# The last norm of a transformer layer: weights multiplied on VectorE before the row factor, the factor applied on ScalarE

## The chip, the cores and the metric

The kernel runs on one core of a Trainium2 chip. The metric is the device time of one execution in microseconds (us), as the median of several runs. Within a core TensorE (PE in the profile) multiplies matrices into PSUM, VectorE (DVE), ScalarE (ACT) and GpSimd (POOL) do elementwise work, SyncE (SP) issues the transfers. Each engine takes its instructions strictly in the order of its own queue, and engines wait for each other by semaphores.

## The reference

One layer of an encoder on two sequences (a prompt and a sample) of 512 rows by 1024 columns. What matters here is the end: the second half of the MLP, a gated residual add, and the final RMS norm.

```python
x = x + g2 * (jnp.square(jax.nn.relu(h @ w_mlp1)) @ w_mlp2)
return rms_norm(x, final_g)      # (x * rsqrt(mean(x*x, -1) + 1e-6)) * final_g
```

`g2` is one gate value per column and sequence, `final_g` one weight per column. The norm therefore multiplies each element by a factor of its row (known only once the whole row is finished) and by a weight of its column (known from the start).

## The kernel before

The product with `w_mlp2` is done by a seven-product scheme on 2x2 blocks, so the output is split into four quarters (i, j): i picks a half of the rows, j a half (512) of the columns. Each row half has four tiles of 128 rows, t = 0..3; tiles 0 and 1 belong to the prompt, 2 and 3 to the sample. In the program's last group of steps the products come in the order P1, P2, P6, P7, P4, P5, P3. The quarter (0,0) is complete after P2, (1,0) after P4, (1,1) after P5 and (0,1) after P3.

Each factor is split into a high and a low part: `prep` casts the high parts on ScalarE (line 841) and subtracts them on VectorE for the low parts (line 842, 128x1024, four of these for a product; `uc` are the left factors, `wc` the right ones). `multiply` (line 1310) then issues 12 matmuls for a product and a row tile, four chunks by three pairs of parts. P1, P6, P5 and P3 run in the PSUM bank pairs `x` (one pair for tiles 0 and 1, one for tiles 2 and 3), P2, P7 and P4 in `y`. The next matmuls into a pair wait until VectorE has read what stood there: (P5, tile 1) waits for the read of (P5, tile 0), (P3, 0) for that of (P5, 1), (P3, 1) for that of (P3, 0), and in the same way for the tiles 2 and 3.

Products that complete no quarter are added into SBUF tiles `acc` (`gather`), and `gated_sums` multiplies these by the gate (line 1349) and adds them to the rows `x2r` (line 1350). A product that completes a quarter goes through `gated_bank`: VectorE reads the bank times the gate into `acc` (line 1356) and adds this to `x2r` (line 1357). `squares` then sums the squares of a tile's 512 columns on ScalarE (line 1362) and GpSimd turns the sum into the mean (line 1365). `finish` has GpSimd raise it to the power -1/2 (line 1369, `rf`), VectorE multiplies each half of the row by the factor and the column weights `fgain` in one instruction (line 1373, SCALAR_TENSOR_TENSOR), and SyncE stores each half (line 1374).

The order of instructions within each engine's queue is set when the kernel is built by a scheduler that goes by dependences and its own costs; at run time it is fixed. So what is written in one place of the code may stand elsewhere in a queue. In the names below, `x2r_0_9503`, `x2r_1_9505`, `x2r_2_9507` and `x2r_3_9509` are the tiles 0 to 3 of row half 1; `x2r_0_9511` to `x2r_3_9517` are those of row half 0. `fgain_9347` are the weights of column half 0, `fgain_9353` those of column half 1. `uc_3` and `wc_3` belong to P7, `uc_5` and `wc_5` to P4, `uc_4` and `wc_4` to P5, `uc_6` and `wc_6` to P3.

Of the kernel before, what the change touches and what calls it, by code (L numbers as in the profile page):

```python
# [12 lines left out]
AF = mybir.ActivationFunctionType  # L13
ALU = mybir.AluOpType

P = 128
# [14 lines left out]
def trunk_kernel(ctx, tc, x0, x1, c0, c1, w_ada, b_ada, norm1_g, w_in, attn_sink, decay_f, decay_b,  # L31
                 w_out, norm2_g, w_mlp1, w_mlp2, final_g, y0, y1):
    nc = tc.nc
    xin = (x0[0], x1[0])
    yout = (y0[0], y1[0])
# [25 lines left out]
    def f2(name, dtype=F32):  # L61
        return work.tile([P, 512], dtype, tag="f2", name=name, bufs=8)

    def junk(name):
        return work.tile([P, 1024], BF16, tag="f2", name=name, bufs=8)

    def small(shape, name, tag="small", bufs=24):
        return work.tile(shape, F32, tag=tag, name=name, bufs=bufs)
# [246 lines left out]
    def x_rstd(b, t, xt):  # L315
        ssq = small([P, 1], f"ssq_{b}_{t}")
        nc.scalar.activation(junk(f"jk_{b}_{t}"), xt, AF.Square, accum_out=ssq)
        return rms_rstd(ssq, f"x_{b}_{t}")
# [511 lines left out]
    P1, P2, P6, P7, P5, P4, P3 = range(7)  # L830
# [9 lines left out]
    def split_to(hi, lo, src):  # L840
        nc.scalar.copy(hi, src)  # L841
        nc.vector.tensor_sub(lo, src, f(hi))  # L842
# [21 lines left out]
    class FirstPair:  # L864
# [15 lines left out]
        def prep(self, p):  # L880
            r1, r2 = self.raw
            c = lambda t: t.rearrange("p (s k n) -> p s k n", s=2, n=P)
            w = lambda t: t.rearrange("p (k n) -> p k n", n=256)
            F1, F2 = slice(0, P), slice(P, 256)
            if p in (P1, P2):
                t = c(self.pair(f"a{p}", True))
                split_to(t[:, 0], t[:, 1], (r1 if p == P1 else r2)[:, :, F1])
                self.left[p] = t[:, 0], t[:, 1]
            elif p == P6:
                self.s1 = f2(f"ws1_{self.n}").rearrange("p (k n) -> p k n", n=P)  # L890
                nc.vector.tensor_tensor(self.s1, r1[:, :, F2], r2[:, :, F2], ALU.add)
                nc.vector.tensor_sub(r1[:, :, F2], r1[:, :, F1], r1[:, :, F2])
                nc.vector.tensor_sub(r1[:, :, F1], self.s1, r1[:, :, F1])
                h, l = w(self.pair("s2h", False)), w(self.pair("s2l", False))
                split_to(h, l, r1)
                self.left[P6] = h[:, :, F1], l[:, :, F1]
                self.left[P7] = h[:, :, F2], l[:, :, F2]
            elif p == P5:
                t = c(self.pair("s1", True))
                split_to(t[:, 0], t[:, 1], self.s1)  # L900
                self.left[P5] = t[:, 0], t[:, 1]
            elif p == P4:
                nc.vector.tensor_sub(r2[:, :, F1], r2[:, :, F1], r1[:, :, F1])
                h, l = w(self.pair("s4h", False)), w(self.pair("s4l", False))
                split_to(h, l, r2)
                self.left[P3] = h[:, :, F1], l[:, :, F1]
                self.left[P4] = h[:, :, F2], l[:, :, F2]
# [162 lines left out]
    r0 = x_rstd(0, 0, xt0[0])  # L1070
# [189 lines left out]
    acc, fin = {}, {}  # L1260
# [65 lines left out]
    def cols_of(j):  # L1326
        return slice(j * 512, (j + 1) * 512)


    def final_loads():  # L1330
        for j in range(2):
            for b in range(NB):
                fin["g", b, j] = f2(f"fgate_{b}_{j}")
                in_order(nc.sync.dma_start(fin["g", b, j], gates[NB + b:NB + b + 1, cols_of(j)].broadcast_to([P, 512])))
            fin["f", j] = f2(f"fgain_{j}")
            in_order(nc.sync.dma_start(fin["f", j], final_g[cols_of(j)].rearrange("(o d) -> o d", o=1).broadcast_to([P, 512])))
# [15 lines left out]
    def gated_bank(q, t, src):  # L1352

        a = acc[q, t // 2][:, t % 2, :]
        x = fin["x", q[0], t][:, cols_of(q[1])]
        nc.vector.tensor_tensor(a, src, fin["g", t // 2, q[1]], ALU.mult)  # L1356
        nc.vector.tensor_tensor(x, x, a, ALU.add)

    def squares(q, t):
        i, j = q  # L1360
        ss = small([P, 1], f"ssf_{i}_{t}_{j}")
        nc.scalar.activation(junk(f"jkf_{i}_{t}_{j}")[:, :512], fin["x", i, t][:, cols_of(j)], AF.Square, accum_out=ss)
        before = fin.get(("ms", i, t), EPS)
        ms = fin["ms", i, t] = small([P, 1], f"msf_{i}_{t}_{j}")
        nc.gpsimd.tensor_scalar(ms, ss, 1.0 / D, before, ALU.mult, ALU.add)

    def finish(i, t):
        r = small([P, 1], f"rf_{i}_{t}")
        nc.gpsimd.tensor_tensor(r, fin["ms", i, t], neghalf[:, 0:1], ALU.pow)
        x = fin["x", i, t]  # L1370
        r0 = i * 256 + (t % 2) * P
        for j in range(2):
            nc.vector.scalar_tensor_tensor(x[:, cols_of(j)], x[:, cols_of(j)], r, fin["f", j], ALU.mult, ALU.mult)
            nc.sync.dma_start(yout[t // 2][r0:r0 + P, cols_of(j)], x[:, cols_of(j)])


    ahead = {P1: lambda: (load_w(0, 0, 0), load_u(0, P1)),
# [26 lines left out]
    def loads(s):  # L1404
        if 2 < s < len(steps):
            load_u(*steps[s])

    def weights(s):
        if 2 < s < len(steps):
            g, p = steps[s]  # L1410
            for k, j in blocks.get(p, ()):
                load_w(g, k, j)

    for s, (g, p) in enumerate(steps[:-2]):
        loads(s + 2)
        weights(s + 3)
        final = g == ng - 1
        if final and p == P1:
            final_loads()
        if s + 1 < len(steps) and s > 0:  # L1420
            prep(*steps[s + 1])
        for t in range(4):
            src = multiply(g, p, t)
            if final and p == P4:
                gated_bank((1, 0), t, src[:, t % 2, :])
                squares((1, 0), t)
            elif t % 2 == 1:
                gather(p, t // 2, src)
        if final:
            if p == P2:  # L1430
                final_rows(1)
                final_rows(0)
            elif p == P6:
                gated_sums((1, 0))
                gated_sums((0, 0))
            elif p == P7:
                gated_sums((1, 1))
                gated_sums((0, 1))
                for t in range(4):
                    squares((0, 0), t)  # L1440
    prep(*steps[-1])
    g = ng - 1
    for p, t in ((P5, 0), (P5, 1), (P3, 0), (P5, 2), (P3, 1), (P5, 3), (P3, 2), (P3, 3)):
        src = multiply(g, p, t)
        q = where[p]
        gated_bank(q, t, src[:, t % 2, :])
        squares(q, t)
        finish(q[0], t)
    lates.close()
    front.close()  # L1450

# [26 lines left out]
```

## Time and profile before

| | |
|---|---|
| runs before | 1161.26 us median of 3 (1159.34 to 1162.54) |
| profiled execution | 1161.89 us, of which its span 1160.1 us |
| busy: PE, DVE, ACT, POOL | 96%, 80%, 43%, 6% of the span |
| granted TensorE clock, mean | 0.992 |
| last group's end on PE | about 1149.7 us |
| last elementwise instruction (line 1373) | starts 1155.44 us, two of them take 1.42 us |

Busy shares are means over the whole program; the change concerns its last 80 us or so. A row of the timeline gives the start, the duration, the engine, the line, the operation and its tiles, and in brackets how long the engine had been idle and what released it. `x5` at the end of a row means that many instructions in a row. One instruction may start before the one ahead of it has ended, so the pitch, from start to start, is somewhat shorter than the duration.

### The profile page before, as it was taken

How to read it: one execution, taken by the hardware profiler on the slowest of the kernel's cores; microseconds unless marked ns; L12 is line 12 of the kernel's file. 1: busy time of each engine (PE TensorE's matmuls, PEld its weight loads, DVE VectorE, ACT ScalarE, POOL GpSimd, SP SyncE). 2: the span in 40 equal slices, each digit the busy share in tenths (PEclk: the TensorE clock that was granted, in tenths of full speed). 3: DMA queues.
4: the chain of work that ended last, by engine and by line, in shares of the span. 5: the costliest groups of instructions: out<-in, count | busy, mean ns of one | idle time of the engine just before them, and what ended most of it. 6: DMA issues, size and time to landing. Idle time of an engine off the chain costs nothing.

```text
span 1160.1 us, 14470 instructions
## 1 busy us (share of the span) xinstructions
PE 1109.4 (96%) x5167; PEld 903.8 (78%) x5167; DVE 933.4 (80%) x1550; ACT 494.0 (43%) x846; POOL 69.0 (6%) x79
## 2 busy tenths in 40 slices
PE   5899999999999999999999999999999999999975
PEld 3578787777888788888788888888778888888854
DVE  5888988978888697689998778866696866968896
ACT  4456765435563234346333333332455333432341
POOL 3620001000000000000000000000000000000012
PEclk9999999999999999999999999999999999999988
DMA  9796677655455489941654455443866364464413
GB/s 289 238 283 211 214 230 272 218 193 190 155 167 199 156 303 333 343 148 46 214 204 155 164 165 189 155 163 103 287 230 237 106 195 137 144 200 139 184 37 145
DMA packets 124112, 224.37 MB, mean 193 GB/s; under 512 B 8500, under 2 KB 59780, under 8 KB 124040
## 3 DMA queue, kind: packets, MB, share of 16 engines
q1 hardware_dynamic: 111144, 217.14, 55.8%
q10 hardware_dynamic: 12544, 6.29, 1.9%
q8 instruction: 40, 0.66, 0.3%
q0 software_dynamic: 352, 0.03, 0.1%
q14 instruction: 32, 0.26, 0.1%
HBM read 152.36 MB, written 71.06 MB: 193 GB/s over the span
## 4 chain that ended last, share of the span: by engine, by line
PE 75%; DVE 11%; DMA 5%; issue 3%; ACT 3%; POOL 2%; SPq 0%; ACTq 0%; DVEq 0%; POOLq 0%
PE px_None L936 12%; PE x L1310 12%; PE py_None L936 9%; PE y L1310 9%; PE po L129 2%; PE po L130 2%; PE po L128 2%; DMA raw_ada_g<-in_w_ada_dram 2%; PE po L429 1%; PE ppt L422 1%; PE psc L396 1%; PE pj_rq L129 1%; PE pj_rq L128 1%; PE pj_rv L128 1%; PE pj_rv L130 1%
## 5 line engine op out<-in xcount | busy, mean ns | idle before, releaser
L841 ACT CAST uc_0h<-ur 128x1024 fp32r<-128x1024 f32 x28 | 29.4, 1050 | 67.9 <-PE x L1310 38.1
L1310 PE MATMUL x<-wc_0l,uc_0h 128*128 128x512 f32 x128 | 50.7, 396 | 5.4 <-DVE wc_0l L842 5.4
L1310 PE MATMUL x<-wc_0h,uc_0h 128*128 128x512 f32 x128 | 50.5, 396 | 3.9 <-DVE acc L1356 3.2
L128 PE MATMUL po<-wh_wo,ms 128*128 128x512 f32 x128 | 50.5, 397 | 1.9 <-ACT ms L761 1.9
L1310 PE MATMUL x<-wc_1h,uc_1h 128*128 128x512 f32 x128 | 50.3, 394 | 1.0 <-ACT wc_1h L841 1.0
L1310 PE MATMUL x<-wc_1l,uc_1h 128*128 128x512 f32 x128 | 50.2, 392 | 0.5 <-DVE wc_1l L842 0.5
L1310 PE MATMUL x<-wc_0h,uc_0l 128*128 128x512 f32 x128 | 50.3, 393 | 0.0
L1310 PE MATMUL x<-wc_1h,uc_1l 128*128 128x512 f32 x128 | 50.1, 391 | 0.0
L129 PE MATMUL po<-wl_wo,ms 128*128 128x512 f32 x128 | 49.8, 391 | 0.3 <-DVE wl_wo L103 0.3
L842 DVE TENSOR_TENSOR uc_0l<-ur,uc_0h 128x1024 fp32r<-128x1024 f32 x28 | 34.2, 1222 | 19.6 <-ACT uc_0h L841 15.9
L130 PE MATMUL po<-wh_wo,ms 128*128 128x512 f32 x128 | 49.6, 390 | 0.0
L255 DVE SCALAR_TENSOR_TENSOR adacc_c<-raw_ada_c,cact,adacc_c 128x512 f32<-128x512 f32 x56 | 39.8, 748 | 6.7 <-DMA raw_ada_c<-in_w_ada_dram 5.7
L841 ACT CAST wc_s4h<-raw_w 128x1024 fp32r<-128x1024 f32 x16 | 16.8, 1053 | 62.8 <-PE px_None L936 46.1
L406 ACT ACTIVATE st<-st,negm 128x256 f32<-128x256 f32 (+1 forms) x64 | 35.2, 556 | 18.8 <-DVE negm L401 18.8
L841 ACT CAST wc_0h<-w 128x1024 fp32r<-128x1024 f32 x24 | 25.2, 1049 | 42.4 <-DVE w L1289 16.3
L255 DVE SCALAR_TENSOR_TENSOR adacc_g<-raw_ada_g,cact,adacc_g 128x512 f32<-128x512 f32 x56 | 40.3, 747 | 2.1 <-DMA raw_ada_g<-in_w_ada_dram 1.8
L842 DVE TENSOR_TENSOR wc_0l<-w,wc_0h 128x1024 fp32r<-128x1024 f32 x24 | 29.3, 1221 | 13.5 <-ACT wc_0h L841 13.4
L936 PE MATMUL py_None<-hch,wc_a 128*128 128x512 f32 x120 | 39.7, 390 | 0.1
L936 PE MATMUL px_None<-hch,wc_a 128*128 128x512 f32 x120 | 39.6, 391 | 0.0
L936 PE MATMUL px_None<-hch,wc_s 128*128 128x512 f32 x120 | 39.4, 389 | 0.0
L1310 PE MATMUL y<-wc_1l,uc_1h 128*128 128x512 f32 x96 | 37.5, 391 | 0.6 <-DVE wc_1l L842 0.6
L1310 PE MATMUL y<-wc_0h,uc_0h 128*128 128x512 f32 x96 | 37.6, 392 | 0.0
(397 smaller groups left out, 3484.8 us busy)
## 6 DMA issues: line engine op xcount, KB each, us to landing
ur<-spill SPq DMA_DIRECT2D x56, 512.0 KB, 4.3
raw_w<-in_w_mlp_dram SPq DMA_DIRECT2D x32, 512.0 KB, 3.8
spill<-s SPq DMA_DIRECT2D x64, 256.0 KB, 3.7
w<-in_w_mlp_dram SPq DMA_DIRECT2D x32, 512.0 KB, 5.4
spill<-u SPq DMA_DIRECT2D x48, 256.0 KB, 2.3
raw_ada_g<-in_w_ada_dram SPq DMA_DIRECT2D x16, 512.0 KB, 4.3
raw_ada_c<-in_w_ada_dram SPq DMA_DIRECT2D x16, 512.0 KB, 4.0
raw_ada<-in_w_ada_dram SPq DMA_DIRECT2D x12, 512.0 KB, 8.8
```

The source lines that it names most:

```text
L128: nc.tensor.matmul(ps, lhs[0], rhs[0], start=start, stop=False)
L129: nc.tensor.matmul(ps, lhs[0], rhs[1], start=False, stop=False)
L130: nc.tensor.matmul(ps, lhs[1], rhs[0], start=False, stop=stop)
L255: nc.vector.scalar_tensor_tensor(acc[b], src, cb, acc[b], ALU.mult, ALU.add)
L396: nc.tensor.matmul(psc[:, :w], qs[hh][:, isl], k_[:, s, j0 * P:j1 * P], start=(s == 0), stop=(s == 1))
L406: nc.scalar.activation(st[hh][:, :w], st[hh][:, :w], AF.Exp, bias=negm[:, hh:hh + 1], scale=0.125, accum_out=den[:, hh:hh + 1])
L422: nc.tensor.transpose(pt[:, hh * P:(hh + 1) * P], st[hh][:, jj * P:(jj + 1) * P], ident)
L429: nc.tensor.matmul(po, va[:, j0 + jj, g].rearrange("p s e -> p (s e)"), pts[jj][:, s, :], start=(jj == 0 and s == 0), stop=(jj == nj - 1 a ...
L841: nc.scalar.copy(hi, src)
L842: nc.vector.tensor_sub(lo, src, f(hi))
L936: self.last = nc.tensor.matmul(bank[:, cs], x[:, k, :], y, start=first and k == 0 and i == 0, stop=last and k == 3 and i == 2, skip_group_ ...
L1310: nc.tensor.matmul(out, u[x][:, i % 2, ts_], w[y][:, i % 2, :], start=first and i == 0 and k == 0, stop=end and i == GP - 1 and k == 2, sk ...
```

## The change

The norm's two multiplications are separated. `gained` multiplies a half row by the column weights on VectorE, as a TENSOR_TENSOR, as soon as that half's sum of squares is taken or its rows are complete, before the row factor exists. The factor is then applied by ScalarE, as an ACTIVATE (Copy) with the factor as its scale, once for each half; only the last half of the last tile takes a TENSOR_SCALAR on VectorE. For column half 1 the weighted rows go to the `acc` tile, so that the squares can be read from `x2r` meanwhile.

```diff
-    def finish(i, t):
+    def gained(q, t, dst):
+
+        nc.vector.tensor_tensor(dst, fin["x", q[0], t][:, cols_of(q[1])], fin["f", q[1]], ALU.mult)
+
+    def finish(i, t, last):
+
+        a = acc[(i, 1), t // 2][:, t % 2, :]
+        gained((i, 1), t, a)
         r = small([P, 1], f"rf_{i}_{t}")
         nc.gpsimd.tensor_tensor(r, fin["ms", i, t], neghalf[:, 0:1], ALU.pow)
-        x = fin["x", i, t]
         r0 = i * 256 + (t % 2) * P
-        for j in range(2):
-            nc.vector.scalar_tensor_tensor(x[:, cols_of(j)], x[:, cols_of(j)], r, fin["f", j], ALU.mult, ALU.mult)
-            nc.sync.dma_start(yout[t // 2][r0:r0 + P, cols_of(j)], x[:, cols_of(j)])
+        for j, src in ((0, fin["x", i, t][:, cols_of(0)]), (1, a)):
+            if j == 1 and last:
+                nc.vector.tensor_scalar(src, src, r, None, ALU.mult)
+            else:
+                nc.scalar.activation(src, src, AF.Copy, scale=r)
+            nc.sync.dma_start(yout[t // 2][r0:r0 + P, cols_of(j)], src)
...
                 for t in range(4):
                     squares((0, 0), t)
+            elif p == P4:
+                for t in range(4):
+                    gained((0, 0), t, fin["x", 0, t][:, cols_of(0)])
     prep(*steps[-1])
+    for t in range(4):
+        gained((1, 0), t, fin["x", 1, t][:, cols_of(0)])
...
-        finish(q[0], t)
+        finish(q[0], t, (p, t) == (P3, 3))
```

VectorE's queue at the end of P6's step, ahead of the low parts for P7 (a minus is a row of before alone, a plus of after alone):

```order
 L1350 TENSOR_TENSOR x2r_0_9511<-x2r_0_9511,acc_0_7810 128x512
 L1350 TENSOR_TENSOR x2r_0_9511<-x2r_0_9511,acc_0_8267 128x512
-L1350 TENSOR_TENSOR x2r_1_9513<-x2r_1_9513,acc_0_7810 128x512
+L1369 TENSOR_TENSOR x2r_0_9511<-x2r_0_9511,fgain_9347 128x512
 L1324 TENSOR_TENSOR acc_0_7963<-x_0_0_9371,acc_0_7963 128x1024
 L842 TENSOR_TENSOR uc_3_0l<-ur_3_0_9423,uc_3_0h 128x1024
```

The first of the new multiplications takes the place of one residual add, and that add now stands 13 rows further down, among the other adds of line 1350 and ahead of all low parts of P4 and P5:

```order
 L1350 TENSOR_TENSOR x2r_2_9507<-x2r_2_9507,acc_1_7989 128x512
 L1350 TENSOR_TENSOR x2r_3_9509<-x2r_3_9509,acc_1_7989 128x512
+L1350 TENSOR_TENSOR x2r_1_9513<-x2r_1_9513,acc_0_7810 128x512
 L1350 TENSOR_TENSOR x2r_2_9515<-x2r_2_9515,acc_1_7837 128x512
 L1350 TENSOR_TENSOR x2r_3_9517<-x2r_3_9517,acc_1_7837 128x512
```

VectorE's queue of before from P3's second low part to the first reads of P5's banks (the last two rows):

```order
L842 TENSOR_TENSOR wc_6_0l<-w_3_11_0_9269,wc_6_0h 128x1024
L1356 TENSOR_TENSOR acc_0_7963<-y_3_0_9627,fgate_0_9343 128x512
L842 TENSOR_TENSOR uc_6_1l<-ur_6_1_9717,uc_6_1h 128x1024
L1357 TENSOR_TENSOR x2r_1_9505<-x2r_1_9505,acc_0_7963 128x512
L1356 TENSOR_TENSOR acc_1_7989<-y_3_1_9653,fgate_0_9345 128x512
L842 TENSOR_TENSOR wc_6_1l<-w_3_11_1_9271,wc_6_1h 128x1024
L1357 TENSOR_TENSOR x2r_3_9509<-x2r_3_9509,acc_1_7989 128x512
L1356 TENSOR_TENSOR acc_0_8036<-x_0_0_9371,fgate_1_9349 128x512
L1356 TENSOR_TENSOR acc_1_8063<-x_0_1_9397,fgate_1_9351 128x512
```

The same stretch of the changed kernel, to the same two rows; three more rows of line 1369, for the tiles 1 to 3 of row half 0, stand right ahead of it:

```order
L1356 TENSOR_TENSOR acc_0_7963<-y_3_0_9627,fgate_0_9343 128x512
L842 TENSOR_TENSOR uc_6_0l<-ur_6_0_9715,uc_6_0h 128x1024
L1357 TENSOR_TENSOR x2r_1_9505<-x2r_1_9505,acc_0_7963 128x512
L1356 TENSOR_TENSOR acc_1_7989<-y_3_1_9653,fgate_0_9345 128x512
L842 TENSOR_TENSOR wc_6_0l<-w_3_11_0_9269,wc_6_0h 128x1024
L1357 TENSOR_TENSOR x2r_3_9509<-x2r_3_9509,acc_1_7989 128x512
L842 TENSOR_TENSOR uc_6_1l<-ur_6_1_9717,uc_6_1h 128x1024
L842 TENSOR_TENSOR wc_6_1l<-w_3_11_1_9271,wc_6_1h 128x1024
L1369 TENSOR_TENSOR x2r_0_9503<-x2r_0_9503,fgain_9347 128x512
L1369 TENSOR_TENSOR x2r_1_9505<-x2r_1_9505,fgain_9347 128x512
L1369 TENSOR_TENSOR x2r_2_9507<-x2r_2_9507,fgain_9347 128x512
L1369 TENSOR_TENSOR x2r_3_9509<-x2r_3_9509,fgain_9347 128x512
```

The reads of P5's banks follow right behind, so seven multiplications by the weights now stand between the first reads of P4's banks and the first read of P5's. On PE the matmuls are the same in number; those of (P5, tile 3) are spread over three gaps between the others (4, 4, 4) in place of two (7, 5).

ScalarE's queue at the end of before holds only sums of squares:

```order
L1362 ACTIVATE jkf_2_1_9917,ssf_2_1_9916<-x2r_2_9507 128x512
L1362 ACTIVATE jkf_1_1_9942,ssf_1_1_9941<-x2r_1_9513 128x512
L1362 ACTIVATE jkf_3_1_9967,ssf_3_1_9966<-x2r_3_9509 128x512
L1362 ACTIVATE jkf_2_1_9992,ssf_2_1_9991<-x2r_2_9515 128x512
L1362 ACTIVATE jkf_3_1_10017,ssf_3_1_10016<-x2r_3_9517 128x512
```

In the changed kernel each of these is followed by the two products with the row factor, which wait for GpSimd's `rf`, and the next tile's squares stand behind them:

```order
L1362 ACTIVATE jkf_1_1_9954,ssf_1_1_9953<-x2r_1_9513 128x512
L1382 ACTIVATE x2r_1_9513<-x2r_1_9513,rf_1_9959 128x512
L1382 ACTIVATE acc_0_8267<-acc_0_8267,rf_1_9959 128x512
L1362 ACTIVATE jkf_3_1_9980,ssf_3_1_9979<-x2r_3_9509 128x512
L1382 ACTIVATE x2r_3_9509<-x2r_3_9509,rf_3_9985 128x512
L1382 ACTIVATE acc_1_8063<-acc_1_8063,rf_3_9985 128x512
L1362 ACTIVATE jkf_2_1_10006,ssf_2_1_10005<-x2r_2_9515 128x512
L1382 ACTIVATE x2r_2_9515<-x2r_2_9515,rf_2_10011 128x512
L1382 ACTIVATE acc_1_8293<-acc_1_8293,rf_2_10011 128x512
L1362 ACTIVATE jkf_3_1_10032,ssf_3_1_10031<-x2r_3_9517 128x512
L1382 ACTIVATE x2r_3_9517<-x2r_3_9517,rf_3_10037 128x512
```

VectorE's queue then ends with the read, the add and the weights of the last tile, and one TENSOR_SCALAR (line 1380); no instruction of it but this last waits for GpSimd. SyncE's 16 stores wait for ScalarE in place of VectorE.

## Prediction

> **What bounds the kernel now.** The page first: its own time 1161.89 us, span 1160.1. I then cut the last 73 us into stages. The columns are busy time and instructions of PE, its weight loads, DVE, ACT and POOL, the clock, and the transfers.
>
> ```profile
> 1087.00:1120.00 33.00, 26.98 (x109) 21.24 (x108) 32.78 (x41) 13.06 (x18) 1.20 (x3) 0.91 0.21 64
> 1120.00:1130.00 10.00, 9.60 (x41) 7.56 (x40) 8.95 (x12) 5.73 (x11) 2.84 (x4) 0.95 0.00 1
> 1130.00:1150.00 20.00, 16.92 (x71) 12.71 (x69) 15.02 (x23) 4.84 (x14) 6.58 (x14) 1.00 0.29 109
> 1150.00:1160.00 10.00, 0.00 (x0) 0.00 (x0) 4.96 (x8) 0.72 (x2) 1.48 (x3) 0.59 0.54 202
> ```
>
> From 1087 to 1120 VectorE is busy 32.78 of 33 us: any instruction put there moves everything behind it. ACT is nearly free, which speaks for the change. Next, who waits for whom from 1110 on (total, times, longest):
>
> ```profile
> PE x L1310 <- DVE wc_0l L842: 5.4, 1, 5.4
> PE x L1310 <- DVE acc L1356: 3.2, 4, 1.8
> DVE x2r L1373 <- POOL rf L1369: 6.7, 5, 1.9
> ```
>
> PE waits 5.4 us for P5's low part and 3.2 us for reads of its banks; VectorE stands 6.7 us in front of the row factor, with the next bank's read queued behind. The timeline places these. VectorE up to the first read of P5's banks:
>
> ```profile
> 1119.20 1.30 DVE L1357 TENSOR_TENSOR x2r<-x2r,acc 128x512 f32<-128x512 f32 x2
> 1120.40 1.23 DVE L842 TENSOR_TENSOR uc_0l<-ur,uc_0h 128x1024 fp32r<-128x1024 f32 x1
> 1123.61 0.69 DVE L1356 TENSOR_TENSOR acc<-y,fgate 128x512 f32<-128x512 f32 x1 [0.68 <-PE y L1310]
> 1126.33 0.69 DVE L1356 TENSOR_TENSOR acc<-y,fgate 128x512 f32<-128x512 f32 x1 [0.29 <-PE y L1310]
> 1126.94 1.22 DVE L842 TENSOR_TENSOR wc_1l<-w,wc_1h 128x1024 fp32r<-128x1024 f32 x1
> 1128.07 0.69 DVE L1357 TENSOR_TENSOR x2r<-x2r,acc 128x512 f32<-128x512 f32 x1
> 1128.67 1.28 DVE L1356 TENSOR_TENSOR acc<-x,fgate 128x512 f32<-128x512 f32 x2
> ```
>
> These give the pitches: 0.60 us for a 128x512 TENSOR_TENSOR (1128.07 to 1128.67), 1.13 for a 128x1024 one (1126.94 to 1128.07), and only 0.97 us of idle time in all. PE in the same stretch and on to its end:
>
> ```profile
> 1115.88 0.79 PE L1310 MATMUL x<-wc_0l,uc_0h 128*128 128x512 f32 x1 [5.42 <-DVE wc_0l L842]
> 1116.47 0.63 PE L1310 MATMUL x<-wc_0h,uc_0l 128*128 128x512 f32 x1
> 1116.90 0.63 PE L1310 MATMUL x<-wc_0h,uc_0h 128*128 128x512 f32 x1
> ...
> 1121.10 0.40 PE L1310 MATMUL y<-wc_0h,uc_0l 128*128 128x512 f32 x1
> ...
> 1128.62 0.39 PE L1310 MATMUL x<-wc_1h,uc_1l 128*128 128x512 f32 x1
> 1129.41 0.50 PE L1310 MATMUL x<-wc_0h,uc_0h 128*128 128x512 f32 x1 [0.40 <-DVE acc L1356]
> ...
> 1134.66 0.47 PE L1310 MATMUL x<-wc_0h,uc_0h 128*128 128x512 f32 x1 [0.65 <-DVE acc L1356]
> 1139.18 0.50 PE L1310 MATMUL x<-wc_0h,uc_0h 128*128 128x512 f32 x1 [0.38 <-DVE acc L1356]
> 1146.70 0.50 PE L1310 MATMUL x<-wc_0h,uc_0h 128*128 128x512 f32 x1 [1.77 <-DVE acc L1356]
> 1147.04 0.39 PE L1310 MATMUL x<-wc_0l,uc_0h 128*128 128x512 f32 x1
> 1147.27 0.40 PE L1310 MATMUL x<-wc_0h,uc_0l 128*128 128x512 f32 x1
> 1149.33 0.39 PE L1310 MATMUL x<-wc_1h,uc_1l 128*128 128x512 f32 x1
> ```
>
> PE's last matmul ends at 1149.72. After the idle 5.42 us the starts lie 0.43 apart (1116.47 to 1116.90) until about 1121.10; after the idle 1.77 us they are at once 0.23 apart. Lastly the end, from all engines:
>
> ```profile
> 1146.17 0.63 ACT L1362 ACTIVATE jkf<-x2r 128x512 bf16<-128x512 f32 x1 [4.86 <-DVE x2r L1357]
> 1147.59 0.55 POOL L1369 TENSOR_TENSOR rf<-msf,neghalf 128x1 f32<-128x1 f32 x1
> 1148.17 4.08 DVE L1373 SCALAR_TENSOR_TENSOR x2r<-x2r,rf,fgain 128x512 f32<-128x512 f32 x6 [0.80 <-POOL rf L1369]
> 1152.17 0.68 DVE L1356 TENSOR_TENSOR acc<-x,fgate 128x512 f32<-128x512 f32 x1
> 1152.88 0.69 DVE L1357 TENSOR_TENSOR x2r<-x2r,acc 128x512 f32<-128x512 f32 x1
> 1153.69 0.63 ACT L1362 ACTIVATE jkf<-x2r 128x512 bf16<-128x512 f32 x1 [5.48 <-DVE x2r L1357]
> 1155.44 1.42 DVE L1373 SCALAR_TENSOR_TENSOR x2r<-x2r,rf,fgain 128x512 f32<-128x512 f32 x2 [1.87 <-POOL rf L1369]
> ```
>
> The last bank is read at 1152.17, 2.45 us after PE's end, because six instructions of line 1373 stand ahead of it.
>
> **The change part by part.** (1) One residual add leaves a place where VectorE waited for PE anyway and goes into the full stretch before 1120; the weights' product that takes its place fits the idle time. So P5's low part, and PE with it, come 0.60 us later: 1116.48 in place of 1115.88.
>
> (2) Seven weights' products now lie ahead of the first read of P5's banks: 7 x 0.60 = 4.2 us. The reads of P4's last banks wait for PE, which is 0.60 later too. Queue by queue: three products from 1121.0 to 1122.8, then the wait for PE's y until 1124.2 (1123.61 + 0.6); read, low part, add to 1126.5; the next y at 1126.9; read, low part, add, two low parts, four products (0.60 + 1.13 + 0.60 + 2 x 1.13 + 4 x 0.60 = 7.0) to 1133.9. The first read of P5 starts there in place of 1128.67, 5.2 us later. PE has nothing else: it is through with its earlier work at 1128.85 + 0.60 = 1129.45 and starts (P5, 1) at 1134.65 in place of 1129.41: +5.2, an idle time of about 5.1 us where it was 0.40.
>
> (3) From there PE has the same 72 matmuls. VectorE no longer waits for the factor, so three of the four waits change: before, 0.65 + 0.38 + 1.77 = 2.8 us. After, four matmuls of (P5, 3) cover the read for (P3, 0) and (P3, 1); (P3, 2) waits about 1.2 for the read of (P5, 3), which stands two instructions behind that of (P3, 1), and (P3, 3) about 0.8 for the read of (P3, 2). Together 2.0: -0.8. PE ends at 1149.72 + 5.2 - 0.8 = 1154.1.
>
> (4) The last bank is read at once, at 1154.2 in place of 1152.17: +2.0. Of the 5.2 us lost, 3.2 are given back by (3) and (4).
>
> (5) ScalarE now holds, for each tile, the squares, a wait for the factor, and two products, and the next squares stand behind. Squares to factor is 1.75 us (1153.69 to 1155.44) and 2.0 where VectorE runs beside GpSimd (1146.17 to 1148.17). For a product of ScalarE by a column of factors the nearest rows are these (two of the timeline, then groups by line):
>
> ```profile
> 1085.60 1.04 ACT L841 CAST uc_0h<-ur 128x1024 fp32r<-128x1024 f32 x1
> 1086.54 0.62 ACT L1362 ACTIVATE jkf<-x2r 128x512 bf16<-128x512 f32 x1
> ...
> L253 ACT ACTIVATE adacc_g<-raw_ada_g,cact 128x512 f32<-128x512 f32 x8 | 5.6, 720 | 7.1 <-DMA raw_ada_g<-in_w_ada_dram 7.1
> L808 DVE TENSOR_SCALAR x<-x,rr_x 128x1024 f32<-128x1024 f32 x8 | 6.0, 753 | 3.9 <-DMA x2s<-x 2.0 <-POOL rr_x L306 2.0
> ```
>
> So 0.72, and about 0.63 from start to start: the cast above runs 1.04 and is followed after 0.94, an overlap of 0.1 that I take over. A tile takes ScalarE 1.75 to 2.0 + 2 x 0.63 = 3.0 to 3.3 us, and the last four, behind (P3, 0) and (P5, 2), which come as a pair, have no room between them. They fall behind VectorE by 0.6 (chain 1.75) to 1.4 us (chain 2.0). I take the middle, +1.0, as both kinds of rows occur. Bounds: zero if ScalarE keeps up, and +2 if every product costs its full 0.72.
>
> (6) At the end two instructions of line 1373 in a row (1.42) become 0.72 on ScalarE beside a TENSOR_SCALAR on VectorE, half the 0.75 of the 128x1024 row above, about 0.4. That is -0.7, or -0.3 if the two stores, now issued together, share the transfer engines; -0.5. Their queue, SyncE's, holds nothing else.
>
> Sum without the clock: +2.0 + 1.0 - 0.5 = +2.5.
>
> (7) The clock. The nearest rows for an idle time of 5.1 us are 5.42 (slow afterwards) and 1.77 (not); 5.1 lies by the first. The slow spell of before took 5.22 us for the twelve starts from 1115.88 to 1121.10, where 12 x 0.23 = 2.7 would do: 2.4 us lost, by its length rather than the work. It falls on (P5, 1), which nothing hides, as VectorE waits for it. Taken: +2.4; the bounds are 0 and 2.5.
>
> Sum: +4.9, so 1166.8 on the profiled execution. That stood 0.63 above the median shown: 1166.2, I say 1166.
>
> [...]
>
> **The rivals.** *The stall without the slow clock.* The same wait, but the matmuls after it at 0.23: 1161.26 + 2.5 = 1163.8. For it: 5.1 is shorter than the one idle time that is seen to slow PE, and nothing between 1.77 and 5.42 is seen. Against: it is far nearer to 5.42. *ScalarE becomes the bound.* Its chains run at 3.3 us and more, products at 0.72 or beside GpSimd delays: 1.5 us on top, 1167.7 with the slow clock. Against: ACT was busy 4.84 of 20 us. *Faster.* The seven products stay hidden: VectorE reaches the read of (P5, 0) before PE has done its other work at 1129.45. Then the 2.8 us of waits fall to 2.0, the 2.45 at the end and 0.5 more are gone: 1161.26 - 3.7 = 1157.5. It decides at 4.2 us of slack in VectorE's queue ahead of 1128.67, and the rows show 0.97; against it. *The change does nothing here*: losses and gains cancel, 1161.3, as when the wait in (2) were 2.5 us shorter; the same rows speak against that.
>
> **How the numbers follow.** Slow clock 0.50, stall without it 0.28, ScalarE bound 0.09, faster 0.06, cancelling 0.07. A measurement tells about 0.3%, 3.5 us, from no change, that is 1157.8 to 1164.7. Slower: nearly all of the first and third and a seventh of the second, 0.61; faster 0.05; the rest, 0.34, the same. The range reaches from 1162.6 (the second case with ScalarE keeping up) to 1168.4 (the third with its bounds); the likeliest alone is 1164.8 to 1167.4.
>
> **What would show it.** Right: PE idle about 5 us in front of (P5, 1) with line 1356 as its releaser; starts 0.43 apart behind it; the last read right at PE's end; ScalarE's last squares late for `rf` of the tile ahead. Wrong: the seven instructions of line 1369 well under 0.60 us each, an idle time there under 3 us, or ACT's products far from 0.63.

## The result and the profile after

| | before | after |
|---|---|---|
| median of 6 runs each, same chip | 1161.11 us (1159.34 to 1165.30) | 1167.49 us (1167.17 to 1169.12) |
| profiled execution, its span | 1161.89, 1160.1 us | 1167.19, 1165.4 us |

The change makes the kernel slower: ratio 1.0052, 95% interval 1.0040 to 1.0064, or 6.4 us by the medians.

Two executions have to be set side by side first. A gather that waits for a bank of PE marks how far the program was; this one stands right behind the first of the new multiplications. Timeline of before, VectorE:

```profile
1087.22 1.22 DVE L1324 TENSOR_TENSOR acc<-x,acc 128x1024 f32<-128x1024 f32 x1 [1.08 <-PE x L1310]
```

The same instruction after the change:

```profile
1085.80 1.22 DVE L1324 TENSOR_TENSOR acc<-x,acc 128x1024 f32<-128x1024 f32 x1 [0.80 <-PE x L1310]
```

The profiled execution of after came there 1.42 us earlier. It came just as much earlier to the gather in front of that multiplication (1080.36 in place of 1081.78), so this first multiplication costs nothing. From here on this is added to its times: the spans differ by 5.3 us, but from this place on by 1165.4 + 1.42 - 1160.1 = 6.7 us, which is near the 6.4 of the medians.

Busy time by stage, after (columns: PE, its weight loads, DVE, ACT, POOL, the clock, transfers):

```profile
1087.00:1120.00 33.00, 26.51 (x105) 20.69 (x104) 33.00 (x43) 12.49 (x20) 1.86 (x3) 0.91 0.22 64
1130.00:1150.00 20.00, 15.11 (x54) 11.56 (x55) 14.25 (x23) 8.64 (x18) 5.32 (x11) 0.83 0.27 100
```

VectorE's last 0.2 us of room ahead of 1120 are gone. From 1130 to 1150 the clock is 0.83 where it was 1.00, and PE is busy for 1.8 us less. Who waits for whom from 1110 on:

```profile
ACT x2r L1382 <- POOL rf L1376: 9.3, 7, 1.9
PE x L1310 <- DVE acc L1356: 7.1, 3, 5.1
```

The 6.7 us that VectorE waited for the factor have become 9.3 us of ScalarE's, and PE's waits for reads of banks went from 3.2 to 7.1 us, 5.1 of them in one place. VectorE up to the first read of P5's banks:

```profile
1119.61 1.89 DVE L1369 TENSOR_TENSOR x2r<-x2r,fgain 128x512 f32<-128x512 f32 x3
1123.20 0.69 DVE L1356 TENSOR_TENSOR acc<-y,fgate 128x512 f32<-128x512 f32 x1 [1.70 <-PE y L1310]
...
1130.54 2.49 DVE L1369 TENSOR_TENSOR x2r<-x2r,fgain 128x512 f32<-128x512 f32 x4
1132.95 1.28 DVE L1356 TENSOR_TENSOR acc<-x,fgate 128x512 f32<-128x512 f32 x2
```

The seven products by the weights stand in two groups, three ahead of P4's reads and four ahead of P5's. PE behind them:

```profile
1115.08 0.79 PE L1310 MATMUL x<-wc_0l,uc_0h 128*128 128x512 f32 x1 [5.42 <-DVE wc_0l L842]
...
1133.68 0.80 PE L1310 MATMUL x<-wc_0h,uc_0h 128*128 128x512 f32 x1 [5.08 <-DVE acc L1356]
...
1137.69 0.61 PE L1310 MATMUL x<-wc_1h,uc_1h 128*128 128x512 f32 x1
1138.12 0.41 PE L1310 MATMUL x<-wc_1l,uc_1h 128*128 128x512 f32 x1
1138.37 0.39 PE L1310 MATMUL x<-wc_1h,uc_1l 128*128 128x512 f32 x1
...
1148.54 0.50 PE L1310 MATMUL x<-wc_0h,uc_0h 128*128 128x512 f32 x1 [1.21 <-DVE acc L1356]
1152.34 0.50 PE L1310 MATMUL x<-wc_0h,uc_0h 128*128 128x512 f32 x1 [0.78 <-DVE acc L1356]
...
1155.00 0.39 PE L1310 MATMUL x<-wc_1h,uc_1l 128*128 128x512 f32 x1
```

After 5.08 us of idle time ten starts lie 0.43 apart, then 0.23 again. Two short waits follow, and PE ends at 1155.39. The end, from all engines:

```profile
1155.42 0.61 ACT L1362 ACTIVATE jkf<-x2r 128x512 bf16<-128x512 f32 x1
1155.43 0.69 DVE L1356 TENSOR_TENSOR acc<-x,fgate 128x512 f32<-128x512 f32 x1 [1.69 <-PE x L1310]
...
1156.15 0.69 DVE L1357 TENSOR_TENSOR x2r<-x2r,acc 128x512 f32<-128x512 f32 x1
1156.22 0.75 POOL L1365 TENSOR_SCALAR msf<-ssf,msf 128x1 f32<-128x1 f32 x1 [2.08 <-ACT jkf L1362]
1156.88 0.69 DVE L1369 TENSOR_TENSOR acc<-x2r,fgain 128x512 f32<-128x512 f32 x1
1157.06 0.92 POOL L1376 TENSOR_TENSOR rf<-msf,neghalf 128x1 f32<-128x1 f32 x1
1158.01 0.72 ACT L1382 ACTIVATE x2r<-x2r,rf 128x512 f32<-128x512 f32 x1 [1.89 <-POOL rf L1376]
...
1159.25 0.61 ACT L1362 ACTIVATE jkf<-x2r 128x512 bf16<-128x512 f32 x1
...
1160.40 0.55 POOL L1376 TENSOR_TENSOR rf<-msf,neghalf 128x1 f32<-128x1 f32 x1
1160.99 0.72 ACT L1382 ACTIVATE x2r<-x2r,rf 128x512 f32<-128x512 f32 x1 [1.03 <-POOL rf L1376]
1160.99 0.49 DVE L1380 TENSOR_SCALAR acc<-acc,rf 128x512 f32<-128x512 f32 x1 [3.42 <-POOL rf L1376]
```

The last bank is read at once. Its row is complete at 1156.84 (1156.15 + 0.69), but the last Square starts at 1159.25: ScalarE first has the Square, the wait for the factor and the products of the tile ahead (1155.42 to 1159.25, 3.83 us). Beside VectorE's lines 1357 and 1369 GpSimd's mean takes 0.75 us and the factor 0.92; beside nothing the two take 0.26 (at 1160.06) and 0.55.

### The profile page after: what moved, and what is told of

Read it like the earlier page. It is cut to its first block, busy times and chain, and to the rows that moved or that the text cites. A ratio compares the mean times of both kernels' runs of the same rounds, so it can differ in the third digit from the quotient of the medians.

```text
span 1165.4 us, 14486 instructions
## 1 busy us (share of the span) xinstructions
PE 1111.6 (95%) x5167; PEld 905.3 (78%) x5167; DVE 933.0 (80%) x1551; ACT 503.7 (43%) x861; POOL 72.1 (6%) x79
## 4 chain that ended last, share of the span: by engine, by line
PE 76%; DVE 11%; DMA 4%; issue 3%; ACT 3%; POOL 2%; SPq 0%; ACTq 0%; POOLq 0%; DVEq 0%
PE x L1310 13%; PE px_None L936 13%; PE py_None L936 9%; PE y L1310 9%; PE po L129 2%; PE po L130 2%; PE po L128 2%; PE po L429 1%; PE ppt L422 1%; PE psc L396 1%; PE pj_rv L128 1%; PE pj_rv L130 1%; PE pj_rv L129 1%; PE pj_rg L128 1%; PE pj_rg L130 1%
## 5 line engine op out<-in xcount | busy, mean ns | idle before, releaser
L1310 PE MATMUL y<-wc_0l,uc_0h 128*128 128x512 f32 x96 | 37.7, 393 | 0.5 <-DVE wc_0l L842 0.5
```

The lines of the kernel that those rows point to most:

```text
L1310: nc.tensor.matmul(out, u[x][:, i % 2, ts_], w[y][:, i % 2, :], start=first and i == 0 and k == 0, stop=end and i == GP - 1 and k == 2, sk ...
```

## The experiments

Theory: the loss has three parts, namely PE's wait with the slow matmuls behind it, caused by the products ahead of P5's reads; ScalarE's queue; and little else. Each kernel was run beside the kernel before, and "+2.9" below is the distance of the two medians there; for the change itself it is +6.4. A step of 0.0010 in the ratio is 1.2 us, so the times alone do not decide between two kernels that lie less than about 2 us apart; there the profiles have to.

| kernel | median, us | before, us | difference | ratio, 95% |
|---|---|---|---|---|
| the change | 1167.49 | 1161.11 | +6.4 | 1.0040 to 1.0064 |
| 1 weights late | 1164.40 | 1161.45 | +2.9 | 1.0008 to 1.0037 |
| 2 idle time filled | 1163.29 | 1161.45 | +1.8 | 0.9997 to 1.0020 |
| 3 filled, order of after | 1165.75 | 1161.28 | +4.5 | 1.0022 to 1.0048 |
| 4 squares paired | 1165.35 | 1161.28 | +4.1 | 1.0021 to 1.0043 |
| 5 no factor products | 1164.73 | 1161.45 | +3.3 | 1.0014 to 1.0036 |
| 6 no products of half 1 | 1165.58 | 1161.45 | +4.1 | 1.0026 to 1.0047 |
| 7 factor on VectorE | 1167.70 | 1161.28 | +6.4 | 1.0041 to 1.0072 |
| 8 weights late and paired | 1162.18 | 1160.84 | +1.3 | 0.9998 to 1.0021 |
| 9 before, tiles held | 1164.04 | 1161.28 | +2.8 | 1.0013 to 1.0030 |
| 10 before, products held | 1162.09 | 1160.84 | +1.3 | 0.9996 to 1.0014 |
| 11 before, reads first | 1160.19 | 1161.92 | -1.7 | 0.9976 to 0.9994 |

**1. The weights late.** The products of the tiles (1, t) by the weights go behind the reads of P5's banks:

```diff
     def finish(i, t, last):
         a = acc[(i, 1), t // 2][:, t % 2, :]
         gained((i, 1), t, a)
+        if i == 1:
+            gained((1, 0), t, fin["x", 1, t][:, cols_of(0)])
...
-    for t in range(4):
-        gained((1, 0), t, fin["x", 1, t][:, cols_of(0)])
```

> The four weights' products of row half 1, column half 0 are traced with the tiles they belong to, behind the reads of P5's banks; the rest of the changed kernel stays. Theory (these products ahead of the first read of P5 make PE wait 5.1 us and then run slowly): the read comes 2.4 us earlier, the idle time is 2.7 us in place of 5.1 and starts behind it lie 0.23 apart at once; 2.4 + 2.1 us less, of which some comes back as ScalarE's queue stays the bound at the end: about 1163.4, some 4 us under the changed kernel. Rival (ScalarE's chain in the last tiles alone makes the loss, the wait on PE is hidden by it): 1 us less at most, 1166.5 or more.

It took 1164.40 us: 3.4 us of the 6.4 are gone, against 4.1 expected, so the place of these four products makes about half of the loss. Timeline of PE:

```profile
1133.14 0.80 PE L1310 MATMUL x<-wc_0h,uc_0h 128*128 128x512 f32 x1 [2.67 <-DVE acc L1356]
```

and its clock (the column behind the busy times) in two stretches of 1 us:

```profile
1132.00:1133.00 1.00, 0.00 (x0) 0.00 (x0) 1.00 (x3) 0.00 (x0) 0.53 (x1) 0.85 0.00 0
1133.00:1134.00 1.00, 0.86 (x2) 0.77 (x3) 1.00 (x3) 0.00 (x0) 0.00 (x0) 0.50 0.00 0
```

The idle time is 2.67 us, as expected, but the starts behind it still lie 0.43 apart: seven in 3.1 us, where 7 x 0.23 = 1.6 would do. These 1.5 us were not expected after so short a wait.

**2. The idle time filled.** Twenty matmuls that nobody reads run on PE while it waits:

```diff
+        if (p, t) == (P5, 1):
+            done[P5, 2] = multiply(g, P5, 2)
+            with tc.issue_after(last_mm[P5, 2].ins):
+                for n in range(20):
+                    idle = nc.tensor.matmul(bank["y", 0][:, 0, :], ...)
...
```

> Twenty matmuls whose results nobody reads fill PE's idle time in front of (P5, tile 1) of the changed kernel; the wait itself stays. Theory (the slow clock after the idle time is a loss of its own, on the path): (P5, 1) starts when it did, its starts lie 0.23 apart, 2.1 us less: about 1165.4. Rival (the clock falls for another reason than PE's idle time, or the slow spell is hidden by ScalarE's queue at the end): no change, 1167.5.

1163.29 us, 2.1 less than expected. The matmuls behind are at 0.23 us again (PE):

```profile
1136.04 0.50 PE L1310 MATMUL x<-wc_0h,uc_0h 128*128 128x512 f32 x1 [0.55 <-DVE acc L1356]
```

But the scheduler had also set ScalarE's queue anew: the squares of (P5, 3) stood ahead of the products of (P3, 1), so the factor's chain of one tile ran beside the other's. Its last Square starts 0.18 us behind its row (1156.76 against 1155.89 + 0.69). Two effects in one kernel, so it decides nothing by itself. The next two part them.

**3. Filled, with ScalarE's order of after.**

```diff
+        if (p, t) == (P5, 3):
+            with tc.issue_after(made["c", 0, 1, 1].ins):
+                squares(q, t)
+        else:
             squares(q, t)
```

> As the kernel with twenty unread matmuls in the idle time, but ScalarE's order held as in the changed kernel (the squares of tile (P5,3) stand behind the factor products of (P3,1)); TensorE and VectorE have the same order as there. Theory (the fill's 4.2 us were about 2 us of clock and wait and about 2 us of ScalarE's order): TensorE stays at 0.23 us from start to start, the last Square starts some 2 us after its bank is read, and the time is about 1165.3. Rival (the clock and the wait alone gave it all): 1163.3.

1165.75 us. PE is as in kernel 2 (`1136.18 0.50`, idle 0.55, then 0.23 apart), and the lag is back. VectorE's row is complete at 1155.99 + 0.69:

```profile
1155.99 0.69 DVE L1357 TENSOR_TENSOR x2r<-x2r,acc 128x512 f32<-128x512 f32 x1
```

and ScalarE's last Square comes 2.41 us later:

```profile
1159.09 0.61 ACT L1362 ACTIVATE jkf<-x2r 128x512 bf16<-128x512 f32 x1
```

So filling the idle time is worth 1.9 us (6.4 - 4.5), where the theory had 2, and each run of this kernel (at most 1167.02 us) is below each run of the change (at least 1167.17). Not all of it is the clock: a few matmuls of (P5, 3) stand elsewhere in PE's queue as well, and one later wait is 0.78 us where it was 1.21.

**4. The squares paired, nothing else.** The changed kernel with the squares of (P5, 3) ahead of the products of (P3, 1) on ScalarE; PE and VectorE have the order of after.

```diff
+        if (p, t) == (P3, 1):
+            continue
+        if (p, t) == (P5, 3):
+            with tc.issue_after(made["s", 1, 3, 1].ins):
+                finish(0, 1, False)
         finish(q[0], t, (p, t) == (P3, 3))
```

> The changed kernel with ScalarE's order alone changed: the squares of tile (P5,3) stand ahead of the factor products of (P3,1), so that the factor's chain of one tile runs beside the other's. Theory (the last Square waits in ScalarE's queue, which holds a factor's wait ahead of each Square): its lag of 2.4 us behind the read of its bank shrinks to under 0.5, TensorE's wait of 5.1 us and the matmuls 0.43 apart stay, and the time is about 1165.3. Rival (the lag is hidden by the stores or by VectorE): 1167.5.

1165.35 us as the theory has it: 2.3 us of the loss were ScalarE's queue, by the medians and by the lag alike. PE's 5.08 us of idle time remain, and the last Square follows its row (1159.07 + 0.69) by 0.09 us. VectorE, then ScalarE:

```profile
1159.07 0.69 DVE L1357 TENSOR_TENSOR x2r<-x2r,acc 128x512 f32<-128x512 f32 x1
```

```profile
1159.85 0.63 ACT L1362 ACTIVATE jkf<-x2r 128x512 bf16<-128x512 f32 x1
```

The parts of kernels 3 and 4 add up, 1.9 + 2.3 = 4.2, to what kernel 2 had at once, 4.5, within the runs' scatter.

**5. No factor products on ScalarE** (but for the last tile's).

```diff
-            else:
+            elif last:
                 nc.scalar.activation(src, src, AF.Copy, scale=r)
```

> The changed kernel without ScalarE's products with the row factor, but for the last tile: the other tiles are stored without the factor. Theory (ScalarE's in-order queue makes the last squares 2.3 us late): they start about 0.15 us after the last residual add, 2.3 us less, 1165.2. Rival (the last squares wait for VectorE and PE only): no change, 1167.5. GpSimd's factor takes 0.9 us where VectorE multiplies beside it: if it is VectorE that slows it, these rows stay at 0.9; if ScalarE, they fall to 0.55.

1164.73 us, and the last Square starts 0.12 us behind its row (1156.52 against 1155.71 + 0.69), as the theory has it. This and the next kernel ask what made the lag. Without the products the factor is still slow where VectorE multiplies beside it, so it is not these products that slow GpSimd (GpSimd's timeline):

```profile
1149.39 1.00 POOL L1376 TENSOR_TENSOR rf<-msf,neghalf 128x1 f32<-128x1 f32 x1
...
1157.69 0.55 POOL L1376 TENSOR_TENSOR rf<-msf,neghalf 128x1 f32<-128x1 f32 x1
```

The changed kernel says the same: its factor at 1146.23 runs beside a product of ScalarE (1145.92 and 1146.55) and takes 0.55 us.

**6. No products by the weights for column half 1 on VectorE**, those that stand right behind each tile's add.

```diff
         a = acc[(i, 1), t // 2][:, t % 2, :]
-        gained((i, 1), t, a)
```

> The changed kernel without the weights' products of column half 1 on VectorE, which stand beside GpSimd's mean and factor in the last tiles: what is stored for this half is not the norm. Theory (VectorE's two-input multiplications beside it slow GpSimd from 0.55 to 0.92 us for a factor, and so lengthen ScalarE's chain from 1.75 to up to 2.6 us for a tile): the chain falls to about 1.75 everywhere, 1.9 us less, 1165.6. Rival (GpSimd is slowed by ScalarE's products): rows of GpSimd and the time stay, 1167.5.

1165.58 us as expected. GpSimd's factor is at 0.55 us for three of the last four tiles, and the last Square starts 0.82 us behind its row (1154.59 + 0.69) in place of 2.41. VectorE, GpSimd and ScalarE:

```profile
1154.59 0.69 DVE L1357 TENSOR_TENSOR x2r<-x2r,acc 128x512 f32<-128x512 f32 x1
```

```profile
1154.28 0.55 POOL L1375 TENSOR_TENSOR rf<-msf,neghalf 128x1 f32<-128x1 f32 x1
```

```profile
1156.10 0.61 ACT L1362 ACTIVATE jkf<-x2r 128x512 bf16<-128x512 f32 x1
```

So 1.6 us of the lag go with VectorE's products beside GpSimd. What is left is the length of ScalarE's queue and one factor that still runs beside an add of line 1357 and takes 0.96 us (at 1150.88).

**7. The factor on VectorE too.** Weights early as in the change, the factor as a TENSOR_SCALAR on VectorE for both halves.

```diff
-            if j == 1 and last:
-                nc.vector.tensor_scalar(src, src, r, None, ALU.mult)
-            else:
-                nc.scalar.activation(src, src, AF.Copy, scale=r)
+            nc.vector.tensor_scalar(src, src, r, None, ALU.mult)
```

> One part alone: the rows are multiplied by the weights on VectorE ahead of the factor, as in the changed kernel, but the factor is applied by VectorE as well (a TENSOR_SCALAR for each half of columns), and ScalarE has no product. Theory (the loss is the weights' products ahead of the first reads of P5's banks): TensorE's wait of about 5 us and its slow matmuls stay, the lag of ScalarE goes, and VectorE waits for the factor ahead of the later reads: about 1167. Rival (what ScalarE got is what was lost): 1164.5 or less.

1167.70 us, the time of the change. Its waits from 1110 on:

```profile
PE x L1310 <- DVE acc L1356: 9.2, 3, 5.1
DVE x2r L1379 <- POOL rf L1376: 6.2, 6, 1.1
```

The move to ScalarE therefore gained nothing in sum: it takes 6.2 us of waits out of VectorE's queue and gives the time back in its own.

**8. Weights late and squares paired**, the edits of kernels 1 and 4 together.

> The changed kernel with two of the losses taken away together: the weights' products of the four tiles (1,t) behind the reads of P5's banks, and ScalarE's squares of (P5,3) ahead of the products of (P3,1). Alone the first gave 3.1 us and the second 2.1 us. Theory (they are terms of one sum, at two places): 1167.5 - 3.1 - 2.1 = 1162.3, with TensorE's wait at 2.7 us and the last Square within 0.5 us of its row. Rival (they cover the same time, so that the larger alone counts): 1164.4.

1162.18 us against 1162.3: the two losses lie behind each other and add up (3.4 + 2.3 = 5.7 by the table, and 5.0 at once). With them out the changed kernel is 1.3 us above the kernel before, an interval that holds no change. Most of the runs' scatter arises ahead of the changed stretch: the gather that was used as a mark above stands anywhere from 1085.80 to 1090.02 in the profiled executions. From that mark to the end of the span kernel 8 takes 73.61 us (1159.9 - 1086.29), the kernel before 72.88 (1160.1 - 1087.22).

**9 to 11. The aim without the change.** The kernel before read its last bank 2.45 us after PE's end, because products that wait for a factor stood ahead of it on VectorE. That can be taken away by order alone. First each tile's whole `finish` was held until VectorE had added the next tile:

```diff
+            with tc.issue_after(added.ins):
+                finish(*held)
+        held = (q[0], t)
-        finish(q[0], t)
```

> The kernel before with each late tile's two products held until VectorE has read and added the next tile's banks, and nothing on ScalarE. Theory (before, VectorE's waits for the factor stand ahead of the next bank's read, and the last bank is read 2.45 us after TensorE is done): the last bank is read at TensorE's end, TensorE's later waits shrink by about 0.8, and the time is about 1158. Rival (the end is bound by the factor's chain and the stores whatever the read does): 1161.3.

1164.04 us, slower where faster was expected. GpSimd's queue, which the hold moved as well, has each factor behind the next tile's mean: here the mean of (P5, 1), then the factor of (P5, 0), which could have been made 3 us before. VectorE waits for it (second fence):

```profile
1134.89 0.26 POOL L1365 TENSOR_SCALAR msf<-ssf,msf 128x1 f32<-128x1 f32 x1 [3.06 <-ACT jkf L1362]
1135.11 0.56 POOL L1369 TENSOR_TENSOR rf<-msf,neghalf 128x1 f32<-128x1 f32 x1
```

```profile
1135.70 1.41 DVE L1373 SCALAR_TENSOR_TENSOR x2r<-x2r,rf,fgain 128x512 f32<-128x512 f32 x2 [1.81 <-POOL rf L1369]
```

PE later waits 2.48 us for a bank (up to 1144.17), and 1 us behind that seven slow starts begin (at 1145.33).

Next the factor was made at once, and only products and stores were held, by a list:

```diff
+    ready = {(1, 1): [(1, 0)], (0, 0): [(1, 1)], (0, 1): [(0, 0)], (1, 3): [(1, 2)],
+             (0, 2): [(0, 1), (1, 3)], (0, 3): [(0, 2)]}
...
+        factor(q[0], t)
+        with tc.issue_after(added.ins):
+            for tile in ready.get((q[0], t), ()):
+                finish(*tile)
```

> The kernel before with the two products of each late tile held behind the next reads of banks on VectorE, but each factor made on GpSimd as soon as its squares are there (in the first trial GpSimd's order put a tile's factor behind the next tile's mean, and VectorE waited 1.15 to 1.81 us for each). GpSimd's and ScalarE's order are those of before; only VectorE's and the stores' order differ. Theory (what the change wanted to remove can be had by order alone): every bank is read as TensorE ends it, TensorE's waits of 1.77 and 0.65 us shrink to about 0.4, the last bank is read within 0.3 us of TensorE's end instead of 2.45 us, VectorE waits only for the last factor: 1161.3 - 2.2 - 1.5 = about 1157.6. Rival (the factor's chain and the stores bound the end whatever the reads do): 1161.3; rival (VectorE waits for each factor as in the first trial): 1164.

1162.09 us, no difference to before, where 1157.6 was expected. PE's queue is not quite that of before either: the matmuls of (P5, 3) are spread over other gaps. The waits for factors are gone but the last. One pair stands in the wrong place: the products of (P3, 0) are ahead of the read of (P5, 3), which is ready. VectorE, then PE:

```profile
1142.37 1.41 DVE L1376 SCALAR_TENSOR_TENSOR x2r<-x2r,rf,fgain 128x512 f32<-128x512 f32 x2
1143.70 0.68 DVE L1356 TENSOR_TENSOR acc<-x,fgate 128x512 f32<-128x512 f32 x1
```

```profile
1144.43 0.50 PE L1310 MATMUL x<-wc_0h,uc_0h 128*128 128x512 f32 x1 [2.53 <-DVE acc L1356]
```

Last, this read was put first:

```diff
-    ready = {..., (0, 1): [(0, 0)], (1, 3): [(1, 2)], (0, 2): [(0, 1), (1, 3)], (0, 3): [(0, 2)]}
+    ready = {..., (1, 3): [(0, 0), (1, 2)], (0, 2): [(0, 1)], (0, 3): [(1, 3), (0, 2)]}
```

> As the kernel before with held products, but the bank of (P5,3) is read and added ahead of the held products of (P3,0) (in the second trial they stood 1.33 us ahead of that read, TensorE waited 2.53 us and five matmuls then started 0.43 us apart). TensorE's, ScalarE's and GpSimd's order are the same as in the second trial. Theory (that one misplaced pair ate the gain): TensorE's wait shrinks by 1.3 us to about 1.2, the matmuls stay at 0.23 us, and the time is 1162.1 - 1.3 - 1.0 = about 1159.7, 1.4 us under the kernel before. Rival (the end is bound elsewhere): 1162.

1160.19 us beside 1161.92: 1.7 us faster than before, ratio 0.9985, interval 0.9976 to 0.9994, the lowest median here. The interval ends close to 1, but from the same mark to the end of the span this kernel takes 71.25 us (1157.2 - 1085.95) against 72.88 before and 72.88 in kernel 10 (1160.9 - 1088.02), which is 1.6 us less. PE's waits of 0.65, 0.38 and 1.77 have become these two, at the full clock, and the last bank is read at 1147.98, 0.03 us after PE's end (1147.56 + 0.39). PE, then VectorE:

```profile
1140.94 0.50 PE L1310 MATMUL x<-wc_0h,uc_0h 128*128 128x512 f32 x1 [1.21 <-DVE acc L1356]
1144.93 0.50 PE L1310 MATMUL x<-wc_0h,uc_0h 128*128 128x512 f32 x1 [0.98 <-DVE acc L1356]
```

```profile
1147.98 0.69 DVE L1356 TENSOR_TENSOR acc<-x,fgate 128x512 f32<-128x512 f32 x1 [1.06 <-PE x L1310]
...
1152.49 1.41 DVE L1376 SCALAR_TENSOR_TENSOR x2r<-x2r,rf,fgain 128x512 f32<-128x512 f32 x2 [0.44 <-POOL rf L1369]
```

Part of the gain is lost again at the end. From the last Square to its products it takes 2.97 us (1149.52 to 1152.49) where it had been 1.75, because the held products of two other tiles now run on VectorE beside GpSimd's last mean (1.10 us) and factor (0.94).

## Why the prediction was right, step by step

The time lies in the range, 1.5 us above the forecast, and the direction and the mechanism are those forecast. Every step can be read in the profile; "measured" has the 1.42 us added.

| step | predicted | measured | from |
|---|---|---|---|
| (1) P5's low part, PE's start on P5 | +0.60 | +0.62 | 1115.08 to 1115.88 |
| (2) PE's start on (P5, 1) | +5.2 | +5.7 | 1133.68 to 1129.41 |
| (3) waits of PE after that | -0.8 | -0.8 | 1.21 + 0.78 to 2.80 |
| (7) slow matmuls | +2.4 | +2.1 | ten starts in 4.44 us, 2.3 would do |
| (4) last bank's read, all so far | +4.4 | +4.7 | 1155.43 to 1152.17 |
| (5) last Square behind its row | +1.0 | +2.3 | 2.41 to 0.12 |
| (6) products and stores at the end | -0.5 | -0.25 | -0.70 and +0.45 |
| sum | +4.9 | +6.7 | |

The term that was mis-sized is (5). The prediction took Square to factor as 1.75 to 2.0 us and so 3.0 to 3.3 us for a tile; the last tiles took 3.3 to 3.8. ScalarE's products were as priced, 0.63 from start to start and 0.72 long. What was longer is GpSimd's part, and it goes with the change itself: it puts an add and a product by the weights on VectorE right beside each mean and factor on GpSimd, where 0.26 and 0.55 us become up to 0.75 and 0.92 in the last tiles. Square to factor is 2.59 us in the tile before the last (1155.42 to 1158.01), not 2.0. The price stood in the trace of before: the factors at 1148.48 and 1149.81 took 0.86 us beside line 1373. Kernel 5 shows that the cause is not ScalarE's products, kernel 6 that it goes with VectorE's products, kernel 4 that the lag is worth 2.3 us and can be had back by order. This is in part the rival "ScalarE becomes the bound", which named GpSimd's delays and 1.5 us on top; it got a chance of 0.09, and its time of 1167.7 is nearer to the result than the likeliest. The chance was set by ACT's small busy share, and a share says nothing about a queue in which every Square stands behind a wait.

How long GpSimd's factor took goes with what ran on VectorE beside it: 0.89 to 1.00 us beside lines 1369 and 1357, which read two SBUF tensors (1153.25 and 1149.90 of the changed kernel, 1149.39 of kernel 5, 1150.88 of kernel 6), 0.55 beside no instruction of VectorE (1160.40 of the changed kernel), and 0.55 in kernel 10 beside line 1356, one of whose two inputs is a PSUM bank (the factor at 1143.99).

In (2) most of the extra 0.45 us is there at P4's first bank: it was read at 1124.62 (1123.20 + 1.42), where 1124.2 had been reckoned, because PE's first slow spell lasted longer, 6.08 us (1115.08 to 1121.16) for 5.22; behind it the queue ran as reckoned. This part varies: in the profiles of kernels 4 to 7, which have the same queues up to there, PE starts (P5, 1) 46.7 to 47.1 us behind the mark, in the change 47.9 and before 42.2, so the loss is 4.5 to 4.9 us there, and 5.2 lies between. PE's earlier work ends at 1129.01 in before (1128.62 + 0.39), not at 1128.85, but the sum does not use it. In (6) the two halves of the last tile are stored at the same time, and from the products' end to the span's end it took 3.69 us (1161.71 to 1165.4) where it had been 3.24 (1156.86 to 1160.1). In (7) the choice of the slow clock was right: slow starts follow the wait of 5.08 us in the change and in kernels 4 to 7. They cost 2.1 us in the change and 1.5 to 1.7 in the other four (seven or eight starts). The rival "stall without the slow clock" is refuted by the starts 0.43 apart, "faster" and "cancelling" by the 5.08 us of PE's wait.

One premise of (7) was wrong, that the trace of before shows nothing between 1.77 and 5.42. This holds for its last 73 us alone. At its beginning PE waits 2.13 us, and the clock of the four microseconds from 66 is 0.57. Timeline of before, PE, and its busy times:

```profile
65.20 0.28 PE L229 MATMUL pmt<-ident,mr 4*128 4x4 f32 x2 [2.13 <-ACT mr L221]
```

```profile
66.00:70.00 4.00, 4.00 (x20) 2.54 (x19) 3.04 (x9) 0.14 (x1) 2.38 (x2) 0.57 1.15 346
```

The chances of 0.50 and 0.28 were the author's estimate; read with this row, the second case, the stall without the slow clock, would have had less than its 0.28.

The part of the change that was to help did help: the last read went from 2.45 us behind PE's end to 0.04. But VectorE was hardly relieved: it has 16 products by the weights, 0.60 us from start to start, where it had 16 products of line 1373 at 0.67 (six from 1148.17 to 1152.17), about 1 us less in all. Kernel 7 shows that ScalarE's part in it was worth nothing in sum, and kernel 11 that the gain can be had without any move of arithmetic.

What stays open is the remaining 1.3 us of kernel 8; its interval holds no difference. Its profile still has PE's wait of 2.67 us with slow starts behind it (at 1131.16), and no kernel took that away. Nor is it shown why GpSimd takes longer beside lines 1357, 1369 and 1373 (0.86 to 1.00 us for a factor in place of 0.55); the same program with the weights in another memory was not tried.

## What to carry to other kernels

Work that is known early is free only where its engine has room: 4.2 us of products put into a queue with 1 us of slack came out at the far end as PE's idle time, plus 2.1 us of slow matmuls on top. An engine with a small busy share can still be late when each of its instructions that others need stands behind a wait in its queue, and pairing two tiles' chains by order took 2.3 us of that back. When waits for a late value stand ahead of reads that free a bank, try the order first (reads first, products behind them, the value itself never held): here the third order tried gave 1.7 us, where multiplying early and on a free engine lost 6.4.

## What the runs showed of the hardware

The clock fell after a much shorter idle time than 5.42 us in one execution here, and not after the same one in another. Line 216, near the program's beginning, is the same in all kernels here. Timeline of PE and busy times of before:

```profile
35.85 0.28 PE L216 MATMUL pm<-wl_ada,c 128*4 128x256 f32 x1 [1.77 <-DVE wl_ada L1001]
```

```profile
37.00:41.00 4.00, 4.00 (x22) 3.01 (x20) 3.93 (x5) 0.79 (x2) 3.61 (x2) 1.00 0.39 113
```

The same of kernel 10:

```profile
36.33 0.28 PE L216 MATMUL pm<-wl_ada,c 128*4 128x256 f32 x1 [1.77 <-DVE wl_ada L1001]
```

```profile
37.00:41.00 4.00, 4.00 (x19) 2.56 (x18) 3.96 (x4) 0.79 (x2) 4.00 (x2) 0.62 0.31 71
```

After the same wait of 1.77 us the clock stays at 1.00 in one execution and reads 0.62 in the other. The slow spells that were read from the clock column lasted 3.4 or 6.8 us: in before it reads 0.64, 0.50, 0.50 and 0.65 from 66 to 70, which makes 3.4 us at half the clock, and 0.59 and six times 0.50 from 1114 to 1121, 6.8 us; in kernel 4 it reads 0.58, 0.50, 0.50 and 0.72 in the microseconds from 1137 to 1141, 3.4 us; in the change 0.66, six times 0.50 and 0.93 from 1131 to 1139, 6.8 us, after the same idle time of 5.08 us. The spells began at different distances from PE's work. In kernel 1 PE was idle for 2.67 us and the granted clock is 0.85 in the microsecond from 1132.0, then 0.50: it fell some 2.2 us after PE's last matmul ended (1133.14 - 2.67 = 1130.47), and seven starts were slow. In kernels 9 and 10 idle times of 2.48 and 2.53 us were followed by matmuls at 0.23 us, and slow ones came only 1.2 and 1.9 us later (from 1145.33 and 1146.31).

Between matmuls, idle times of 1.77 us (kernel 10), 2.13 and 5.42 (before), 2.48 (kernel 9), 2.53 (kernel 10), 2.67 (kernel 1) and 5.08 us (the change) were followed by a slow spell; 1.77 us at 35.85 and at 1146.70 and 1.94 us at 405.59 of before were not, as the clock there is 1.00. What decides between them was not shown.

A one-column operation on GpSimd cost 0.26 (the mean at 1160.06 of the changed kernel) or 0.55 us (the factor at 1160.40) alone, and up to 1.54 (the mean at 1120.01 there) and 1.00 (the factor at 1149.39 of kernel 5) where line 1369 ran on VectorE beside it.
